# Transposes of the first and the last head on TensorE, and the gated output written over z

## The chip, the cores and the metric

The kernel runs on one core of one Trainium2 chip. What counts is the time of one execution on the device in microseconds (us). The number for the kernel before is the median of three runs.

## What is computed

One layer of a decoder for 1024 prompt rows and 8 decode rows, D = 1024, 8 heads of 128, in float32. Only the part that the change touches is shown; the rest (a conformer branch, a merge, a convolutional feed-forward) surrounds it.

```python
q, k, v = split_cols(silu(causal_dwconv(qkv)))
q = l2norm(q); k = l2norm(k)
def step(s, xc):                         # chunk after chunk, state s
    qg_c, kg_c, u_c, w_c, qk_c, gl_c = xc
    v_new = u_c - w_c @ s
    o = qg_c @ s + qk_c @ v_new
    s = s * gl_c + kg_c.T @ v_new
    return s, o
o = o * rsqrt(mean(o * o) + EPS) * delta_norm_w
o = o * silu(z)
y_a = o.reshape(b, t, V_DIM) @ w_o_delta
```

## The kernel before

The big products (`gemm`, its matmul at L187) run on TensorE (PE). Weights and activations are split in a high and a low float32r part, three products for each of eight k-slices, so a tile of 344 rows is 24 matmuls; three tiles make one projection of 128 columns. They go through two PSUM buffers `mm`. The projections come in a fixed order: for each head k, q, v (`kT`, `qT`, `vT`), with z, gate and conformer projections between; after head 7's the last z and gate projections; then the output projection of the gated heads, called wod here (`mm<-og`), which takes the split heads `og` as its moving operand, head by head along k.

PE runs in the order in which the program is written. VectorE (DVE), ScalarE (ACT), GpSimd (POOL) and SyncE (SP) run in an order that a scheduler makes. The work on the heads is written as background jobs, Python generators. `tick()` advances them all by a step after every four gemm matmuls, so `yield n` stands for 2n ticks, or 8n matmuls. Where the program must have a job's result (`wait_x`, `finish`), it ticks with no gemm between: such a place is called a bare stretch here.

The job of one head has these parts:

- `delta_a` (L645): the product of keys with themselves (L673), then a 32-step triangular solve on DVE (tiles `xt`, `xx`), whose result `xr` goes through DRAM (`d_x`) and comes back as `dt`. The generator then yields, 26 for head 0, 21 for heads 1 to 6, 14 for head 7.
- `delta_q` (L723): the product of queries with keys (L738) and the sum of squares of q over its columns.
- `delta_b` (L748): transposes of v and k, scaled into `vs` and `kt`; the inverse of a triangular matrix in blocks, of which the first (L776) needs `dt`; and the chain over the eight chunks (L819 to L844), which keeps one output tile `oo` for all heads and waits until the head before is "done".
- `delta_c` (L850): scales `oo`, transposes it, and multiplies it by silu(z) (`zT`) into `oo`; the result goes to DRAM (`d_og`). Head 7's is split at once for wod. A single buffer holds `zT`; the next head's z projection (`z_next`) waits for "done" too.

Four transposes of [128, 1024] for each head go through `flip` (L626): DVE turns blocks of 32x32 (a stream transpose) into tile `ty`, POOL sends it to DRAM (`d_t`), and four POOL transfers bring it back as `tv`. `ty` and `tv` share one buffer. PE's small products of these jobs use three PSUM buffers `tr`.

Of the kernel before, what the change touches and what calls it, by code (L numbers as in the profile page):

```python
# [8 lines left out]
F32 = mybir.dt.float32  # L9
# [7 lines left out]
P = 128  # L17
# [49 lines left out]
def body(tc, I, O):  # L67
# [13 lines left out]
    def stt(out, a, s, b, op0, op1):  # L81
        nc.vector.scalar_tensor_tensor(out=out, in0=a, scalar=s, in1=b, op0=op0, op1=op1)  # L82
# [5 lines left out]
    with top:  # L88
# [545 lines left out]
                nc.gpsimd.dma_start(tv[HB * b:HB * (b + 1)].rearrange("p (a x) -> p a x", a=4), dv[b])  # L634
            return tv.rearrange("p (a c s) -> p c a s", a=4, c=NC)

        def sumsq(src, ss):
            tv = flip(src)
            yield 3
            for c in range(NC):  # L640
                jk = hp.tile([P, P], F32, tag="jk", name="jk")
                nc.scalar.activation(jk.rearrange("p (a s) -> p a s", a=4), tv[:, c], AF.Square,
                                     accum_out=ss[:, c:c + 1])

        def delta_a(X):  # L645
# [71 lines left out]
            for b in range(4):  # L717
                nc.sync.dma_start(dt[HB * b:HB * (b + 1)].rearrange("p c r -> p (c r)"),
                                  d_x[:, b].rearrange("i c r -> i (c r)"))
            yield 14 if h == NH - 1 else 26 if h == 0 else 21  # L720
            X.update(dt=dt, d_x=d_x)

        def delta_q(X):  # L723
            h, kT, qT = X["h"], X["kT"], X["qT"]
            while "sc" not in X:
                yield
            pt = X["pt"]
            brk, c1, nc1g, rqs = X["sc"]
            gr2 = hp.tile([P, NC, P], F32, tag="gr", name="gr2")
            nc.sync.dma_start(gr2.rearrange("p c i -> p (c i)"),  # L730
                              d_gc[1, h * NC:(h + 1) * NC].rearrange("c i -> (c i)").unsqueeze(0).broadcast_to([P, T]))
            yield 3
            for half in range(2):
                g = trp()
                gv = g.rearrange("p (c i) -> p c i", i=P)
                for i in range(4):
                    c = half * 4 + i
                    nc.tensor.matmul(gv[:, i, :], kT[:, cs[c]], qT[:, cs[c]], start=True, stop=True)  # L738
                mul(pt[:, 4 * half:4 * half + 4, :], gv, pt[:, 4 * half:4 * half + 4, :])
                yield  # L740
            ss = hp.tile([P, NC], F32, tag="ss", name="ss")
            yield from sumsq(qT, ss)
            nc.vector.tensor_scalar(out=rqs, in0=ss, scalar1=EPS, scalar2=EPS / QS ** 2, op0=ALU.add, op1=ALU.mult)
            mul(qT, qT, gr2.rearrange("p c i -> p (c i)"))
            X.update(qdone=True)

        def delta_b(X):
# [5 lines left out]
            kt = hp.tile([P, NC, P], F32, tag="kt", name="kt")  # L753
            vs = hp.tile([P, NC, P], F32, tag="vs", name="vs")
            for src, dst, scl in ((vT, vs, brk), (kT, kt, eg[:, h, :])):
                tv = flip(src)
                yield 5
                for c in range(NC):
# [50 lines left out]
                nc.scalar.copy(tt[0:64, :, 64:128], t2v[0:64])  # L809
            X["merged"] = True  # L810
            yield 2
            while h > 0 and not Xs[h - 1].get("done"):
                yield
            S = None
            oo = hp.tile([P, NC, P], F32, tag="oo", name="oo")
# [34 lines left out]
        def delta_c(X):  # L850
# [11 lines left out]
            for c in range(NC):  # L862
                nc.scalar.activation(oo[:, c, :], oo[:, c, :], AF.Copy, scale=f[:, c:c + 1])
            yield 2
            tv = flip(oo.rearrange("p c i -> p (c i)"))
            yield 7
            zv, ov = zT.rearrange("p (c b r) -> p b c r", b=4, r=HB), oo.rearrange("p c (b r) -> p b c r", b=4)
            for b in range(4):
                stt(ov[:, b], tv[:, :, b], dnw, zv[:, b], ALU.mult, ALU.mult)
            if h == NH - 1:  # L870
                og = oo.rearrange("p c i -> p (c i)")
                for o in (0, 512):
                    split(oghi[h][:, o:o + 512], oglo[h][:, o:o + 512], og[:, o:o + 512])
            yield
            if h < NH - 1:
                nc.sync.dma_start(d_og[h], oo.rearrange("p c i -> p (c i)"))
            X["done"] = True

        def decode(h, sq_):
            nc.sync.dma_start(O["qs"][h], sq_)  # L880
# [849 lines left out]
```

## Time and profile before

| | us |
|---|---|
| median of three runs (lowest, highest) | 1848.58 (1846.51, 1850.22) |
| the profiled execution | 1842.05 |
| its span | 1840.3 |
| PE busy | 1774.9 |
| DVE busy | 1403.6 |
| ACT busy | 894.0 |
| POOL busy | 215.5 |

The busy times are those of one profiled execution; they overlap. PE is busy for 96% of the span, so what matters is when PE is idle, and for whom it waits. The profile gives for every instruction its start, its duration and, if its engine was idle before, for how long and what ended that. Matmuls overlap, so the step from one start to the next is PE's pace, not the duration of one.

### The profile page before, as it was taken

The page shows a single profiled execution, that of the slowest core. Times are in us where ns is not written, and L with a number is a line of the kernel's source. Part 1 is how long each engine was busy: PE and PEld are TensorE (multiplying, and loading weights), DVE is VectorE, ACT ScalarE, POOL GpSimd, SP SyncE. Part 2 cuts the span into 40 slices and gives each one's busy share as a digit, 9 for nine tenths or more (in the row PEclk, how much of TensorE's full clock was granted, in tenths as well). Part 3 has the DMA queues.
Part 4 walks back from the last instruction along what each step waited for, and adds up shares of the span by engine and source line. Part 5 has one row for each costly group of instructions (what it writes and reads, how often), then busy time and mean ns, then how long its engine had stood idle before and what let it go on. Part 6 is the DMA issues. An engine that isn't in the chain of part 4 may idle for free.

```text
span 1840.3 us, 35347 instructions
## 1 busy us (share of the span) xinstructions
PE 1774.9 (96%) x13075; PEld 1751.9 (95%) x13075; DVE 1403.6 (76%) x3296; ACT 894.0 (49%) x2110; POOL 215.5 (12%) x409
## 2 busy tenths in 40 slices
PE   7997999999999999989899998999999999999997
PEld 7897999999999999989899998999999999999997
DVE  7998699789978997745428578988778878856553
ACT  5564566565655656444203344444444445644432
POOL 5422121113021211100000000100000000100000
PEclk9999999999999999989999999999999999999998
DMA  4164345434544454544547732322222224767562
GB/s 165 59 181 141 92 128 168 147 119 144 153 144 122 143 171 149 159 132 147 184 140 228 239 114 94 108 81 72 90 76 75 87 75 150 241 211 227 169 184 84
DMA packets 161741, 257.38 MB, mean 140 GB/s; under 512 B 40544, under 2 KB 88992, under 8 KB 161568
## 3 DMA queue, kind: packets, MB, share of 16 engines
q1 hardware_dynamic: 143760, 213.10, 37.3%
q0 software_dynamic: 10752, 33.56, 5.8%
q10 hardware_dynamic: 7056, 8.47, 1.3%
q8 instruction: 102, 1.67, 0.4%
q14 instruction: 71, 0.58, 0.1%
HBM read 189.14 MB, written 65.92 MB: 139 GB/s over the span
## 4 chain that ended last, share of the span: by engine, by line
PE 66%; DVE 3%; DMA 2%; ACT 1%; issue 1%; SPq 0%; DVEq 0%; ACTq 0%
PE mm L187 25%; PE mm L1334 23%; PE mm L1599 13%; PE psS L834 0%; PE po L841 0%; DMA og<-d_og 0%; PE po L831 0%; PE pv L825 0%; DVE l_t L79 0%; PE pk L820 0%; PE nrm_b L224 0%; PE tr L673 0%; DMA yl<-d_y 0%; PE tr L738 0%; DMA d_ch<-c 0%
## 5 line engine op out<-in xcount | busy, mean ns | idle before, releaser
L187 PE MATMUL mm<-hhi,whi 128*128 128x344 f32 x1360 | 450.7, 331 | 11.9 <-ACT whi L85 6.6
L187 PE MATMUL mm<-hhi,wlo 128*128 128x344 f32 x1360 | 450.3, 331 | 2.7 <-DVE wlo L79 2.7
L187 PE MATMUL mm<-hlo,whi 128*128 128x344 f32 x1360 | 441.2, 330 | 0.0
L187 PEld LDWEIGHTS mm<-hhi,whi 128*128 128x128 f32 x1360 | 261.1, 192 | 16.1 <-ACT whi L85 7.0
L187 PEld LDWEIGHTS mm<-hhi,wlo 128*128 128x128 f32 x1360 | 261.3, 192 | 5.1 <-DVE wlo L79 3.9
L187 PEld LDWEIGHTS mm<-hlo,whi 128*128 128x128 f32 x1360 | 259.3, 192 | 0.5
L1334 PE MATMUL mm<-l_t,uhi 128*128 128x258 f32 x704 | 200.4, 285 | 1.4 <-DVE l_t L79 1.4
L1334 PE MATMUL mm<-h_t,uhi 128*128 128x258 f32 x704 | 200.4, 285 | 0.0
L1334 PE MATMUL mm<-h_t,ulo 128*128 128x258 f32 x704 | 199.4, 283 | 0.0
L82 DVE SCALAR_TENSOR_TENSOR cacc<-u,ccw,cacc 128x512 f32<-128x512 f32 x240 | 174.2, 744 | 0.5 <-ACT cacc L570 0.5
L1599 PE MATMUL mm<-yl,wdh 128*128 128x344 f32 x528 | 168.8, 320 | 0.0
L1599 PE MATMUL mm<-yh,wdh 128*128 128x344 f32 x528 | 168.8, 320 | 0.0
L1599 PE MATMUL mm<-yh,wdl 128*128 128x344 f32 x528 | 168.6, 319 | 0.0
L79 DVE TENSOR_TENSOR wdl<-draw,wdh 128x512 fp32r<-128x512 f32 x144 | 92.0, 646 | 81.4 <-ACT wdh L85 78.0
L145 ACT CAST whi<-wraw 128x512 fp32r<-128x512 f32 x164 | 95.7, 625 | 111.3 <-PE mm L187 93.9
L85 ACT CAST wdh<-draw 128x512 fp32r<-128x512 f32 x144 | 83.2, 584 | 111.8 <-PE mm L1599 103.2
L1334 PEld LDWEIGHTS mm<-l_t,uhi 128*128 128x128 f32 x704 | 133.9, 190 | 2.2 <-DVE l_t L79 2.2
L1334 PEld LDWEIGHTS mm<-h_t,uhi 128*128 128x128 f32 x704 | 133.6, 190 | 0.5 <-DVE u L79 0.2
L1334 PEld LDWEIGHTS mm<-h_t,ulo 128*128 128x128 f32 x704 | 133.5, 190 | 0.0
L187 PE MATMUL mm<-og,whi 128*128 128x344 f32 x512 | 124.6, 323 | 5.6 <-ACT og L85 5.6
L146 DVE TENSOR_TENSOR wlo<-wraw,whi 128x512 fp32r<-128x512 f32 x160 | 107.9, 688 | 13.9 <-ACT whi L145 12.6
L85 ACT CAST uhi<-s 128x512 fp32r<-128x512 f32 x92 | 56.9, 621 | 106.1 <-PE mm L1334 101.7
(356 smaller groups left out, 4287.7 us busy)
## 6 DMA issues: line engine op xcount, KB each, us to landing
draw<-in_wdn SPq DMA_DIRECT2D x120, 256.0 KB, 2.7
raw<-in_wup SPq DMA_DIRECT2D x92, 256.0 KB, 2.8
d_t<-ty POOLq DMA_DIRECT2D x32, 512.0 KB, 3.1
tv<-d_t POOLq DMA_DIRECT2D x128, 128.0 KB, 3.1
yl<-d_y SPq DMA_DIRECT2D x21, 516.0 KB, 5.5
d_y<-av SPq DMA_DIRECT2D x21, 512.0 KB, 3.1
gr<-d_gc SPq DMA_DIRECT2D x16, 512.0 KB, 3.5
wraw<-in_wout SPq DMA_DIRECT2D x32, 256.0 KB, 2.9
```

The lines of the kernel that those rows point to most:

```text
L79: nc.vector.tensor_tensor(out=out, in0=a, in1=b, op=ALU.subtract)
L82: nc.vector.scalar_tensor_tensor(out=out, in0=a, scalar=s, in1=b, op0=op0, op1=op1)
L85: nc.scalar.copy(hi, x)
L145: nc.scalar.copy(hi[:, k:k + 4], raw)
L146: weng["e"].tensor_tensor(out=lo[:, k:k + 4], in0=raw, in1=hi[:, k:k + 4].bitcast(F32), op=ALU.subtract)
L187: nc.tensor.matmul(ps, lhs[:, k, :], r(k), start=k == 0 and i == 0, stop=k == kt - 1 and i == 2)
L1334: nc.tensor.matmul(z[:, b, 0:Q], w[:, k, :], r[b][nm][:, k, :], start=start and n == 0, stop=n == 3 * KH - 1, skip_group_check=True)
L1599: nc.tensor.matmul(ps, w[:, f % KH, :], y[:, f % 3, :], start=h == 0 and n == 0, stop=h == 1 and n == 3 * (NF - 3 * KH) - 1)
```

## The change

Heads 0 and 7: the transposes of q, v, k and the gated output are PE transposes against the identity, into `tr` buffers (a new helper `turn`, four blocks of 128x128 for each half; the output in four quarters of two). ACT and DVE read them from PSUM. Heads 1 to 6 keep `flip`, but the gated output is written over `zT` and sent to DRAM from there. `oo` counts as free three yields after the flip was issued, and the next chain waits for "free" in place of "done". The yield at the end of `delta_a` is 2 longer for heads 1 to 7.

```diff
+        def turn(src):
+            for half in range(2):
+                g = trp()
+                gv = g.rearrange("p (c i) -> p c i", i=P)
+                for i in range(4):
+                    nc.tensor.transpose(gv[:, i, :], src[:, cs[half * 4 + i]], ident)
+                yield half, gv
+
-        def sumsq(src, ss):
+        def sumsq(src, ss, h):
+            if h in (0, NH - 1):
+                for half, gv in turn(src):
+                    for i in range(4):
+                        c = half * 4 + i
+                        jk = hp.tile([P, P], F32, tag="jk", name="jk")
+                        nc.scalar.activation(jk, gv[:, i, :], AF.Square, accum_out=ss[:, c:c + 1])
+                    yield 2
+                return
             tv = flip(src)
             yield 3
...
-            yield 14 if h == NH - 1 else 26 if h == 0 else 21
+            yield 16 if h == NH - 1 else 26 if h == 0 else 23
...
             for src, dst, scl in ((vT, vs, brk), (kT, kt, eg[:, h, :])):
+                if h in (0, NH - 1):
+                    for half, gv in turn(src):
+                        for i in range(4):
+                            c = half * 4 + i
+                            nc.scalar.activation(dst[:, c, :], gv[:, i, :], AF.Copy, scale=scl[:, c:c + 1])
+                        yield
+                    X["vt"] = True
+                    continue
                 tv = flip(src)
                 yield 5
...
-            while h > 0 and not Xs[h - 1].get("done"):
+            while h > 0 and not Xs[h - 1].get("free"):
                 yield
...
-            tv = flip(oo.rearrange("p c i -> p (c i)"))
-            yield 7
-            zv, ov = zT.rearrange("p (c b r) -> p b c r", b=4, r=HB), oo.rearrange("p c (b r) -> p b c r", b=4)
-            for b in range(4):
-                stt(ov[:, b], tv[:, :, b], dnw, zv[:, b], ALU.mult, ALU.mult)
-            if h == NH - 1:
-                og = oo.rearrange("p c i -> p (c i)")
-                for o in (0, 512):
-                    split(oghi[h][:, o:o + 512], oglo[h][:, o:o + 512], og[:, o:o + 512])
-            yield
+            if 0 < h < NH - 1:
+                tv = flip(oo.rearrange("p c i -> p (c i)"))
+                yield 3
+                X["free"] = True
+                yield 4
+                zv = zT.rearrange("p (c b r) -> p b c r", b=4, r=HB)
+                for b in range(4):
+                    stt(zv[:, b], tv[:, :, b], dnw, zv[:, b], ALU.mult, ALU.mult)
+                yield
+                nc.sync.dma_start(d_og[h], zT)
+                X["done"] = True
+                return
+            for qr in range(4):
+                g = trp()[:, 0:256]
+                gv = g.rearrange("p (c i) -> p c i", i=P)
+                for i in range(2):
+                    c = qr * 2 + i
+                    nc.tensor.transpose(gv[:, i, :], oo[:, c, :], ident)
+                og = oo[:, 2 * qr:2 * qr + 2, :].rearrange("p c i -> p (c i)")
+                sl = slice(256 * qr, 256 * qr + 256)
+                stt(og, g, dnw, zT[:, sl], ALU.mult, ALU.mult)
+                if h == NH - 1:
+                    split(oghi[h][:, sl], oglo[h][:, sl], og)
+                yield
             if h < NH - 1:
                 nc.sync.dma_start(d_og[h], oo.rearrange("p c i -> p (c i)"))
-            X["done"] = True
+            X["free"] = X["done"] = True
```

The new rows on PE are 64 transposes. Counted in gemm matmuls issued so far, of which 4104 precede wod, head 0's stand at 476 and 492 (q), 516 and 524 (v), 532 and 540 (k), and 1132 to 1156 (output); head 7's at 3500 and 3516, 3656 and 3664, 3672 and 3680, and 4072, 4080, 4088 and 4096. L776 and the chain of heads 1 to 6 stand 16 matmuls later than before; L776 of heads 0 and 7 stands where it was.

Three places show how the change moves work. The first is DVE at the end of head 0's triangular solve. The fence is the order before; `xr` is the solve's result, `qT`, `vT`, `jk` and `am` belong to head 1, `Sb` to the decode rows.

```order
L73 TENSOR_TENSOR xt_1303<-ab_1236,xx_1241 128x24
L677 SCALAR_TENSOR_TENSOR jk_1984,ss_1931<-tr_1979,const_71 128x128
L79 TENSOR_TENSOR xx_1241<-xx_1241,xt_1303 128x24
L82 SCALAR_TENSOR_TENSOR Sb_1181<-Sb_1181,adec_106,vb_1743 128x128
L73 TENSOR_TENSOR xt_1303<-ab_1236,xx_1241 128x16
L677 SCALAR_TENSOR_TENSOR jk_1986,ss_1931<-tr_1979,const_71 128x128
L79 TENSOR_TENSOR xx_1241<-xx_1241,xt_1303 128x16
```

And the same place in the changed kernel:

```order
L73 TENSOR_TENSOR xt_1307<-ab_1236,xx_1241 128x8
L79 TENSOR_TENSOR xx_1241<-xx_1241,xt_1307 128x8
L729 COPY xr_1617<-xx_1241 128x256
L82 SCALAR_TENSOR_TENSOR qT_1814<-raw_1903,cqw_84,qT_1814 128x344 x3
L693 SCALAR_TENSOR_TENSOR jk_1940,ss_1934<-tr_1935,const_71 128x128
```

The products `jk` of head 1 stood between the last steps of the solve; now they, and three of head 1's `qT` steps, stand behind `xr`. Between the first step of the solve and `xr` 17 instructions fewer are left: 7 `jk`, 6 `qT`, 1 `vT`, 4 `cacc` (conformer convolution), the stream transpose of k, an `am` and a `pt` are gone from there, and 4 small ones have come in. Ahead of the first step little changes: the stream transposes of q and v and 2 `wlo` are gone, 4 `cacc` and a `pt` have come in.

The second place is PE where head 7's chain begins, at the start of the last z projection (a bare stretch). Before:

```order
L795 MATMUL tr_10263<-const_71,tt_123 64x64 x8
L797 MATMUL tr_10264<-tt_123,am_9065 64x64 x8
L807 MATMUL tr_10289<-z2_10282,t1_10281 64x64 x8
L187 MATMUL mm_10311<-hhi0_78,whi_9868 128x344
L187 MATMUL mm_10311<-hhi0_78,wlo_9869 128x344
```

And in the changed kernel:

```order
L819 MATMUL tr_10272<-const_71,tt_123 64x64 x8
L821 MATMUL tr_10273<-tt_123,am_9041 64x64 x8
L831 MATMUL tr_10294<-z2_10291,t1_10290 64x64 x8
L849 MATMUL pv_10310<-vs_9989,tt_123 128x128
L187 MATMUL mm_10327<-hhi0_78,whi_9862 128x344
```

The chain's first product `pv` stood 12 gemm matmuls further on; now it follows at once on the product whose copy `tt` it reads. On ACT the copies `oo<-po` of chunk 0 stood behind the second `zT<-mm` of this projection and now stand ahead of the first; those of chunk 1 stood behind the second and now stand behind the first.

The third place is DVE ahead of wod, where head 7's gated output is made. Before:

```order
L82 SCALAR_TENSOR_TENSOR c_10733<-c_10733,ccv_86,tr_11104 128x258 x4
L146 TENSOR_TENSOR wlo_11144<-wraw_11145,whi_11143 128x512
L146 TENSOR_TENSOR wlo_11144<-wraw_11149,whi_11143 128x512
L593 COPY c_11128<-cdec_104 128x4x8
L82 SCALAR_TENSOR_TENSOR oo_10324<-tv_11091,dnw_87,zT_10300 128x8x32 x4
L79 TENSOR_TENSOR og_10937<-oo_10324,og_10936 128x512 x2
```

And in the changed kernel:

```order
L79 TENSOR_TENSOR og_10926<-oo_10308,og_10925 128x256
L82 SCALAR_TENSOR_TENSOR oo_10308<-tr_11132,dnw_87,zT_10316 128x256
L79 TENSOR_TENSOR og_10926<-oo_10308,og_10925 128x256
L146 TENSOR_TENSOR wlo_11152<-wraw_11153,whi_11151 128x512
L146 TENSOR_TENSOR wlo_11152<-wraw_11157,whi_11151 128x512
L593 COPY c_11173<-cdec_104 128x4x8
```

The multiplications by silu(z) stood behind a copy into `c` (conformer); all four quarters now stand ahead of it.

## Rows read from the trace of the kernel before

**Rows 1.** The page's first part, for one engine: busy time, its share of the span, instructions.

```profile
PE 1774.9 (96%) x13075; PEld 1751.9 (95%) x13075; DVE 1403.6 (76%) x3296; ACT 894.0 (49%) x2110; POOL 215.5 (12%) x409
```

**Rows 2.** PE's waits over the whole span: the line that waited, what it waited for, us in total, times, the longest.

```profile
PE tr L776 <- DMA dt<-d_x: 12.6, 4, 9.4
...
PE po L831 <- ACT oo L844: 6.0, 2, 5.1
PE mm L187 <- ACT og L85: 5.6, 1, 5.6
```

**Rows 3.** One window of 25 us at head 0's first wait: its length, busy time and instructions of PE, weight loads, DVE, ACT and POOL, then the granted clock (1 is 2.4 GHz, 0.5 is 1.2 GHz), the DMA engines' share and GB/s.

```profile
175.00:200.00 25.00, 19.06 (x186) 17.59 (x187) 12.74 (x42) 14.03 (x50) 2.92 (x8) 0.80 0.41 121
```

**Rows 4.** The timeline of PE around head 0's L776 and the start of its chain: start, us, engine, line, operation, how many, and in brackets the idle time before and what ended it.

```profile
169.57 0.32 PE L187 MATMUL mm<-hhi,wlo 128*128 128x344 f32 x1
169.72 0.32 PE L187 MATMUL mm<-hlo,whi 128*128 128x344 f32 x1
179.45 1.39 PE L776 MATMUL tr<-dt,am 32*32 32x32 f32 x32 [9.40 <-DMA dt<-d_x]
...
181.22 0.49 PE L187 MATMUL mm<-hhi,wlo 128*128 128x344 f32 x1
...
184.66 0.49 PE L187 MATMUL mm<-hhi,wlo 128*128 128x344 f32 x1
...
188.78 0.63 PE L795 MATMUL tr<-const,tt 64*64 64x64 f32 x8
...
193.38 0.49 PE L825 MATMUL pv<-vs,tt 128*128 128x128 f32 x2 [0.99 <-ACT tt L809]
193.71 1.06 PE L738 MATMUL tr<-qT,kT 128*128 128x128 f32 x8
194.60 0.39 PE L834 MATMUL psS<-vn,kt 128*128 128x128 f32 x2
```

**Rows 5.** The timeline of DVE and of SP's queue on the way to head 0's `dt`: the three stream transposes, the solve's result, and the loads of `dt`.

```profile
98.49 1.23 DVE L629 STREAM_TRANSPOSE ty<-qT 128x1024 f32<-128x1024 f32 x1
...
118.45 1.25 DVE L629 STREAM_TRANSPOSE ty<-vT 128x1024 f32<-128x1024 f32 x1
...
136.22 1.25 DVE L629 STREAM_TRANSPOSE ty<-kT 128x1024 f32<-128x1024 f32 x1 [1.70 <-ACT vs L759]
...
170.65 0.38 DVE L713 COPY xr<-xx 128x256 f32<-128x256 f32 x1
...
175.78 2.28 SPq L718 DMA_DIRECT2D dt<-d_x  x4
```

**Rows 6.** The timeline around the start of head 7's chain, all engines: head 6's gated output on DVE and SP, the chain on PE, ACT's copies.

```profile
776.16 0.98 ACT L863 ACTIVATE oo<-oo,f 128x128 f32<-128x128 f32 x3
...
788.06 1.25 DVE L629 STREAM_TRANSPOSE ty<-oo 128x1024 f32<-128x1024 f32 x1 [4.45 <-ACT kt L759]
...
800.88 0.40 PE L187 MATMUL mm<-hhi,whi 128*128 128x344 f32 x1
801.12 0.32 PE L187 MATMUL mm<-hhi,wlo 128*128 128x344 f32 x1
...
803.13 1.14 ACT L957 CAST og<-og 128x512 fp32r<-128x512 f32 x2 [5.11 <-DMA og<-d_og]
...
803.23 1.67 DVE L82 SCALAR_TENSOR_TENSOR oo<-tv,dnw,zT 128x256 f32<-128x256 f32 x4
...
803.28 0.39 PE L825 MATMUL pv<-vs,tt 128*128 128x128 f32 x2
...
804.92 0.32 SPq L876 DMA_DIRECT2D d_og<-oo  x1
...
808.05 0.28 ACT L843 ACTIVATE oo<-po 128x128 f32<-128x128 f32 x1 [0.97 <-DMA d_og<-oo]
...
808.77 0.79 PE L831 MATMUL po<-S,qT 128*128 128x128 f32 x2 [5.10 <-ACT oo L844]
...
809.65 0.49 PE L187 MATMUL mm<-hhi,wlo 128*128 128x344 f32 x1
...
813.08 0.36 PE L187 MATMUL mm<-hhi,wlo 128*128 128x344 f32 x1
```

**Rows 7.** The timeline at the start of wod, PE and DVE: the last matmul ahead of the wait, what DVE did, the first matmul behind it.

```profile
875.63 0.32 PE L187 MATMUL mm<-og,whi 128*128 128x344 f32 x1
...
879.03 0.18 DVE L593 COPY c<-cdec 128x32 f32<-128x32 f32 x1 [3.14 <-DMA d_ch<-c]
...
879.21 1.67 DVE L82 SCALAR_TENSOR_TENSOR oo<-tv,dnw,zT 128x256 f32<-128x256 f32 x4
...
881.59 0.66 PE L187 MATMUL mm<-og,whi 128*128 128x344 f32 x1 [5.64 <-ACT og L85]
...
884.77 0.36 PE L187 MATMUL mm<-og,wlo 128*128 128x344 f32 x1
```

**Rows 8.** Groups by line and form over the whole span: line, engine, operation, form and count, then busy us, mean ns of one, idle time before.

```profile
L759 ACT ACTIVATE vs<-tv,sc 128x128 f32<-128x128 f32 x64 | 21.3, 397 | 2.2 <-DMA tv<-d_t 2.2
...
L920 PE MATMUL tr<-const,vnd 128*8 128x128 f32 x8 | 2.2, 272 | 0.0
```

**Rows 9.** PE's waits at L776 in the windows 300 to 400 and 600 to 700, the columns as in rows 2.

```profile
PE tr L776 <- DMA dt<-d_x: 0.8, 1, 0.8
...
PE tr L776 <- DMA dt<-d_x: 2.5, 2, 2.0
```

More of the change, by code (lines that the diff above doesn't have):

```diff
@@ L741, in delta_q @@
             ss = hp.tile([P, NC], F32, tag="ss", name="ss")
-            yield from sumsq(qT, ss)
+            yield from sumsq(qT, ss, h)
             nc.vector.tensor_scalar(out=rqs, in0=ss, scalar1=EPS, scalar2=EPS / QS ** 2, op0=ALU.add, op1=ALU.mult)
```

## The prediction

> **What bounds the kernel now.** I read the page's first part, then PE's waits, then the timeline around the longest of them, then DVE, ACT and the queues there. PE is busy for 96% of the span [rows 1], so the change can gain only where PE waits or runs slowly, and loses wherever it gives PE work. Three waits are within reach of the change: one of 9.40 us for head 0's `dt`, one of 5.10 at `po` for ACT's copy of `oo`, one of 5.64 for head 7's split output; beside the 9.40, L776 waits 3.2 in all [rows 2], for later heads [rows 9].
>
> Behind each wait PE runs slowly for a while. Behind the first, the gemm's step is 0.287 us (181.22 to 184.66, 12 steps), against 0.15 to 0.16 ahead of it (169.57 to 169.72), and L776 takes 1.39; the granted clock of that window is 0.80 [rows 3, 4]. The step at half speed, 0.287, less the full one, 0.158, makes 0.129 lost on each matmul. Between the wait and the return of full speed stand some 14 matmuls behind the first wait, 10 behind the second (809.65 to 813.08, with three chain products) and 11 behind the third (to 884.77) [rows 4, 6, 7]. So the waits cost more than their length.
>
> **Stall 1: head 0's `dt`.** `dt` is `xr` sent out and loaded again: `xr` at 170.65, the loads issued from 175.78, L776 free at 179.45 [rows 4, 5]. PE was done with its gemm at about 170.0, so `dt` must come 9.4 us sooner, or PE come later. Both happen. Between the first step of the solve and `xr` DVE loses 21 instructions and gains 4 small ones, by the order. DVE has no gap there but the 1.70 us at the stream transpose of k, which waits for ACT to free the one `ty` buffer [rows 5]. That stream transpose takes 1.25, the gap goes with it; the other 20 at an estimated 0.45 each (from 1.25 for 1024 columns [rows 5], and 0.3 to 0.6 for a quarter or half of that) make 9; the four small ones give back about 0.8. Sum: 1.25 + 1.70 + 9 − 0.8, about 11 us sooner. The lower bound counts the stream transposes and the gap alone, 1.23 + 1.25 + 1.25 + 1.70 = 5.4; below that, nothing, if DVE is held elsewhere. I take 11, since the order shows where the rest went: behind `xr`. On its side PE has head 0's six halves of q, v and k to do first, about 3.1 us (below). `dt` then lands at about 168.5, PE comes at 173.1: the wait is gone with 4.6 us of margin. Gain: 9.40 + 0.7 (L776 takes 1.39 against an estimated 0.7 at full speed) + 14 × 0.129 = 1.8, together **11.9**. What is late next on PE is the chain's own copy wait of 0.99 at 193.38 [rows 4], which stays.
>
> **The transposes on PE.** Twelve halves of four and eight quarters of two, 64 blocks. The nearest row is eight records of f32 products of the same size, 193.71 to 194.60, 0.111 us each; such a product of two records between gemm matmuls also delays the next one, whose step is 0.24 (800.88 to 801.12) in place of 0.158, so 0.08 for each group [rows 4, 6]. A transpose in this kernel has one record where a product has two (L920, one for each head) [rows 8]. So a half costs 4 × 0.111 + 0.08 = 0.52, a quarter 0.30: 12 × 0.52 + 8 × 0.30 = **8.7** (6.2 + 2.4). The upper bound is two records each, 64 × 0.111 = 7.1 more. A floor lies at 64 × 0.07 (the eight transposes of 64 columns take 0.56 or so [rows 4]): 2.6 less. I take 8.7, since the columns are 128.
>
> The halves also need buffers: three `tr` in turn, freed by ACT's four reads of each half at about 0.40 [rows 8], 1.6 us; two halves stand 8 matmuls apart, 1.27 + 0.52 = 1.8 us, for v and k. ACT just keeps up where it has nothing else to do. Bounds: nothing, to 12 × 1.6 = 19. I take **2**, since two buffers stand between a half and its reuse.
>
> **Stall 2: head 6's output and head 7's chain.** The 5.10 at 808.77 has this history: ACT's `oo<-po` waits until `d_og<-oo` has been sent (issued 804.92, ACT free at 808.05), that waits for `oo<-tv` at 803.23, and the stream transpose of `oo` ran only at 788.06 because head 7's k held the `ty` buffer (4.45 idle for ACT's `kt`) [rows 6]. The change takes away each link: head 7's k no longer uses `ty`; `oo` is read last by the stream transpose; and chunk 0's copies stand ahead of `zT<-mm` on ACT. Gone: 5.10 + 10 × 0.129 = 1.3 + about 0.7 for L831, L834 and L841 at half speed: **7.1**. Against it, head 7's `pv` now follows at once on L831's product and waits for ACT's copy `tt`; the same wait for head 0 is 0.99 [rows 4]: **1.0** lost. What is queued behind it on PE is the whole z projection.
>
> `zT` is now what is held: until `d_og<-zT` has been sent, 3.1 us from issue to ACT's release [rows 6]. The scale of head 6's `oo` ended at 777.1, and comes 16 matmuls later by the order, 2.5 us: 779.6. The stream transpose follows at once, or where DVE came to it before, 788.06 less its 4.45 idle, 783.6, and 2.5 later: 786.1. From there to the multiplication it was 15.2 us (788.06 to 803.23), and 1.7 + 3.4 more free `zT`: 799.9 to 806.4. PE needs the first of its two `mm` buffers back for the third z tile; that stood at the `pv` of chunk 1, 803.28 [rows 6], and now 1.0 later. So PE waits 0 to 2.6; I take **1.0**. ACT's cast of `og`, which waited 5.11 for its load at 803.13 [rows 6], stands ahead of chunk 1's `vn`; that may cost 0 to 2.
>
> **Stall 3: wod.** The 5.64 at 881.59 is for `og` of head 7; DVE's multiplication at 879.21 stood in line behind the copy L593, which waited 3.14 for `d_ch<-c` [rows 7]. In the new order all four quarters stand ahead of L593, and the last PE quarter 8 matmuls ahead of wod, 29 matmuls or 4.6 us ahead of the first use. Gone: 5.64 + 11 × 0.129 = **7.0**. L593 now holds only the evacuation of wod's first tile; for that, and for a late quarter, I take **1.0** off, bounds 0 to 2.
>
> **Heads 1 to 6.** Their L776 stands 16 matmuls later, 2.5 us; the waits of 0.8 and of 2.5 in two pieces [rows 9] are covered almost wholly: **3.0**, bounds 0 to 5 with the clock behind them. The chain's later start costs nothing there: the next head's z comes long after.
>
> **Sum.** 11.9 + 7.1 − 1.0 − 1.0 + 7.0 − 1.0 + 3.0 = 26.0 gained, 8.7 + 2 = 10.7 lost: 15.3 in all. From the profiled execution that is 1842.05 − 15.3 = 1826.8. This execution was 6.5 us below the median of the runs, which is the number that counts: 1848.58 − 15.3 = **1833**.
>
> **A rule on the clock.** Behind the eight transposes at 188.78 the products run at 0.111 each, as at full speed [rows 4]. The Trainium skill (TensorE: Matmul & The Clock Gate, Part 4: PE-mode transpose) says that a transpose does not count as busy for the clock as a product does, and gives some 275 ns for one in a kernel; 64 such end to end would be an estimated 17.6 us in place of 8.7, and the sum 1842. By the trace it doesn't hold for eight blocks of 64 columns; for groups of four blocks of 128 no row shows it.
>
> **The rivals.** First, `zT` takes the place of `oo`: `d_og<-zT` lands after 809, ACT holds chunk 1's copies behind `zT<-mm`, and stall 2's net 5.1 is not gained: 1838. For it, the length of the path from the stream transpose (15.2); against it, the span worked out above, which ends before. Second, head 0's `dt` comes no sooner, because DVE is held by something ahead of the solve: then PE's 3.1 us go into the wait for nothing and the 11.9 aren't gained, 1833 + 8.8 = 1842. For it, DVE's order ahead of the solve hardly changes; against it, 21 instructions gone behind. Third, the clock falls at the turns of heads 0 and 7: 64 matmuls from the first to the last of head 0's and 24 of head 7's v and k at 0.129 make 11.4: 1845. Fourth, the slower side: the `tr` buffers bind. ACT answers each half only after PE has come to the third buffer on, 12 × 1.6 = 19 in place of 2, and a transpose takes two records, 7 more: 1833 + 24 = 1857. It decides where ACT's reads of a half come more than about 3.6 us late (two halves on PE); ACT's wait of 5.11 for `og` shows that it can be that late, but that place is not at a turn. That the change would not do what it says is shut out by the order, which has the 64 rows and the moved chain.
>
> **How the numbers follow.** The sum 0.50, first rival 0.17, second 0.13, third 0.05, fourth 0.10, and the first and second together 0.05 (1847). What a measurement of this kernel can tell from no change is about 0.2%, 3.7 us. The sum's own range is 1828 to 1838 from its bounds. The range reaches from 1825 (no wait for buffers, all of stall 3, more clock) to 1845, which leaves out the fourth case and half of the doubled one. Faster: 0.50 + 0.17 + 0.13 and half of the third make 0.82, less a little for the spread of each, 0.79; same 0.10 (the third, the doubled one and that spread); slower 0.11.
>
> **What would show it.** Right: no wait at L776 for head 0 and a granted clock near 1 there; head 7's `po` and wod's eighth head with no wait over 1 us; transposes of 128 columns one record each at about 0.11. Wrong: PE waiting at a transpose for ACT or DVE, `zT<-mm` on ACT waiting for `d_og<-zT`, or a new wait of PE for `vn`.

## The result, and the profile after

The changed kernel takes 1818.8 us, the median of four runs (1814.67 to 1819.69), against 1847.55 for the kernel before (four runs, 1843.89 to 1850.22). The ratio is 0.9841, with a 95% interval of 0.9818 to 0.9865: 25 to 34 us faster. In the experiments, with more runs of the kernel before, the same two kernels gave 0.9865 (0.9846 to 0.9883) and 0.9869 (0.9850 to 0.9889). The forecast was 1833, the range 1825 to 1845: the direction was right, the gain nearly twice the one forecast.

The page's first part, after, against [rows 1]. The span is 22.4 us shorter and PE's busy time only 1.1, although 64 instructions came in: most of what went is idle time, and the rest is slow running behind the waits.

```profile
PE 1773.8 (98%) x13139; PEld 1751.1 (96%) x13139; DVE 1399.4 (77%) x3290; ACT 892.8 (49%) x2112; POOL 188.7 (10%) x369
```

PE's waits over the whole span, after: line, what it waited for, us in total, times, longest. Of [rows 2] the waits for `oo` and for `og` are gone, and that for `dt` (L776, now L800) has shrunk from 12.6 us in four pieces to one of 0.5. What is left in the stretch that the change edits is small and has other causes, most of it ACT's copies of `vn` and `tt` in the chain. The larger waits that the view lists besides, 6.7 for `whi` and 4.9 for `nrm_r`, lie outside that stretch and stood there before.

```profile
PE psS L858 <- ACT vn L852: 2.6, 4, 1.0
...
PE pv L849 <- ACT tt L833: 1.7, 2, 1.0
...
PE tr L809 <- DVE rk L82: 0.9, 1, 0.9
...
PE tr L800 <- DMA dt<-d_x: 0.5, 1, 0.5
```

The timeline of PE, after: a half of head 0's v, turned ahead of gemm matmuls, then L800 of head 0. Four transposes of one record each start 0.11 apart from 118.68 on ((0.60 − 0.27) / 3, with the 0.27 of one record from [rows 8]). The next matmul starts at 119.04, only 0.03 behind the fourth, and its own step is 0.24 in place of 0.16. L800 has no wait (9.40 in [rows 4]) and lasts 0.69 in place of 1.39. The next product, L809, waits 0.94 for DVE.

```profile
118.52 0.32 PE L187 MATMUL mm<-hlo,whi 128*128 128x344 f32 x1
118.68 0.60 PE L642 MATMUL tr<-const,vT 128*128 128x128 f32 x4
119.04 0.40 PE L187 MATMUL mm<-hhi,whi 128*128 128x344 f32 x1
119.28 0.32 PE L187 MATMUL mm<-hhi,wlo 128*128 128x344 f32 x1
...
173.40 0.69 PE L800 MATMUL tr<-dt,am 32*32 32x32 f32 x32
...
177.74 0.69 PE L809 MATMUL tr<-zs,xs 32*32 32x32 f32 x32 [0.94 <-DVE rk L82]
```

Two windows of PE, after: length, busy time and instructions, granted clock, DMA share, GB/s. The first holds head 0's turns of q, v and k (the last ends at 124.4), the second is that of [rows 3], where the clock was 0.80. Both show 1.00.

```profile
109.00:124.00 15.00, 15.00 (x107) 1.00 0.53 155
...
175.00:200.00 25.00, 21.79 (x197) 1.00 0.46 134
```

DVE and SP's queue on the way to head 0's `dt`, after, to be read against [rows 5]: `xr` at 164.14 in place of 170.65, and the loads issued at 168.21 in place of 175.78.

```profile
164.14 0.42 DVE L729 COPY xr<-xx 128x256 f32<-128x256 f32 x1
...
168.21 1.71 SPq L734 DMA_DIRECT2D dt<-d_x  x4
```

The start of head 7's chain, after, against [rows 6]. The stream transpose of head 6's `oo` runs at 770.86, 17.2 us earlier than before (8.1 earlier counted from head 7's L795, which PE reached at 789.33 and now at 780.22), and waits for the scale on ACT, not for `kt`. The multiplication now writes `zT`, and ACT's first `zT<-mm` waits 0.83 for its sending. PE's `po` has no wait; `pv` waits 0.67 for `tt`.

```profile
770.86 1.25 DVE L629 STREAM_TRANSPOSE ty<-oo 128x1024 f32<-128x1024 f32 x1 [1.75 <-ACT oo L887]
...
784.42 0.80 PE L849 MATMUL pv<-vs,tt 128*128 128x128 f32 x2 [0.67 <-ACT tt L833]
...
788.26 1.27 DVE L82 SCALAR_TENSOR_TENSOR zT<-tv,dnw,zT 128x256 f32<-128x256 f32 x3
...
789.55 0.32 SPq L898 DMA_DIRECT2D d_og<-zT  x1
...
792.42 0.39 PE L855 MATMUL po<-S,qT 128*128 128x128 f32 x2
...
794.95 0.46 ACT L529 ACTIVATE zT<-mm 128x344 f32<-128x344 f32 x1 [0.83 <-DMA d_og<-zT]
```

A short slow stretch stays where this chain begins: the clock was granted at half from about 784 to 787 (0.94 over the window 784 to 809), much as from 793 to 796 before. What is gone is the second one, behind the wait at `po`.

The start of wod, after, against [rows 7]: the last quarter's transposes at 855.28, its low part on DVE at 856.66, wod's first matmul with no wait behind it, and the copy L593, which held head 7's output up, behind all of that.

```profile
855.28 0.38 PE L906 MATMUL tr<-const,oo 128*128 128x128 f32 x2
...
856.66 0.42 DVE L79 TENSOR_TENSOR og<-oo,og 128x256 fp32r<-128x256 f32 x1 [0.47 <-ACT og L85]
...
856.77 0.32 PE L187 MATMUL mm<-og,whi 128*128 128x344 f32 x1
...
859.62 0.18 DVE L593 COPY c<-cdec 128x32 f32<-128x32 f32 x1 [0.36 <-DMA d_ch<-c]
```

### The profile page after: what moved, and what is told of

Read it like the earlier page. It is cut to its first block, busy times and chain, and to the rows that moved or that the text cites. A ratio compares the mean times of both kernels' runs of the same rounds, so it can differ in the third digit from the quotient of the medians.

```text
span 1817.9 us, 35374 instructions
## 1 busy us (share of the span) xinstructions
PE 1773.8 (98%) x13139; PEld 1751.1 (96%) x13139; DVE 1399.4 (77%) x3290; ACT 892.8 (49%) x2112; POOL 188.7 (10%) x369
## 4 chain that ended last, share of the span: by engine, by line
PE 85%; DVE 8%; DMA 3%; ACT 2%; issue 1%; SPq 0%; DVEq 0%; ACTq 0%
PE mm L187 41%; PE mm L1372 23%; PE mm L1637 13%; PE psS L858 1%; PE tr L689 1%; PE pv L849 1%; PE po L865 1%; PE pk L844 1%; PE tr L754 1%; PE po L855 1%; DVE xt L82 1%; DMA yl<-d_y 1%; DMA wraw<-in_wout 0%; PE tr L821 0%; PE tr L947 0%
## 5 line engine op out<-in xcount | busy, mean ns | idle before, releaser
L187 PE MATMUL mm<-hhi,whi 128*128 128x344 f32 x1360 | 448.7, 330 | 10.9 <-ACT whi L85 6.7
```

The lines of the kernel that those rows point to most:

```text
L187: nc.tensor.matmul(ps, lhs[:, k, :], r(k), start=k == 0 and i == 0, stop=k == kt - 1 and i == 2)
```

## The experiments

To see where the time went, each profile was cut at points on PE that have the same number of gemm matmuls ahead of them in both kernels. The touched stretch runs from the first product of keys (L673, 95.53 us before) to the first matmul of the conformer's projection (972.58). No edit stands in the program ahead of it or behind it; those parts are called the untouched stages. A head's decode product is the one of its decode rows with ones (`tr<-s,ones`, L895 before). In us, first profiles:

| stretch on PE | before | after | gain | forecast |
|---|---|---|---|---|
| first keys product to head 1's decode product (stall 1, head 0's q, v, k) | 101.89 | 93.65 | 8.2 | 8.8 |
| to head 2's decode product (head 0's output) | 103.20 | 103.44 | -0.2 | -1.2 |
| to head 7's decode product (heads 1 to 6, head 7's q) | 444.21 | 439.89 | 4.3 | 2.0 |
| to the start of head 7's chain, L795 (head 7's v, k) | 44.50 | 46.92 | -2.4 | -2.1 |
| to wod (stall 2, head 7's output) | 83.16 | 76.54 | 6.6 | 3.9 |
| to the conformer's projection (stall 3) | 100.09 | 92.66 | 7.4 | 6.0 |
| touched stretch | 877.05 | 853.10 | 23.9 | 17.4, less 2 for buffers |
| untouched, ahead and behind | 963.25 | 964.80 | -1.5 | 0 |

The variants are the changed kernel with sets of heads in place of its fixed ones: TQ (q, v, k turned on PE), TO (output turned on PE), ZS (stream transpose, output over z); other heads go as before. In the changed kernel these are heads 0 and 7, heads 0 and 7, and heads 1 to 6; the yields are 16 and 23 (before 14 and 21). Head 0 alone, head 7 alone and the write into z alone have the old yields.

```diff
-                if h in (0, NH - 1):
+                if h in TQ:
...
-            if 0 < h < NH - 1:
+            if h in ZS:
                 tv = flip(oo.rearrange("p c i -> p (c i)"))
...
+            if h not in TO:
+                tv = flip(oo.rearrange("p c i -> p (c i)"))
+                yield 7
...
+                X["free"] = X["done"] = True
+                return
```

**The kernel before, a second time** (no edit).

> The kernel before, unchanged, profiled once more. In the two profiles on hand the change gained 22.4 us (spans 1840.3 and 1817.9), but in the medians 28.7. Theory A: the first profiled execution of before was a short one, and others wait longer at the same places (dt of head 0, oo, og), since these waits end with transfers; then this profile shows a span nearer 1846 and the waits of 9.4, 5.1 and 5.6 longer by some 5 us in sum. Theory B: executions differ elsewhere, in places that the change does not touch; then the three waits are within 0.5 us of what they were, whatever the span. Ratio to before 1.000 +- 0.002 in both.

Ratio 1.0001 (0.9989 to 1.0012), span 1844.2. The waits for `dt`, `oo` and `og` were 9.44, 5.64 and 5.13 us, against 9.40, 5.10 and 5.64: two moved by 0.5, one up and one down, and the sum by 0.1. The touched stretch took 875.2 us, the untouched stages 969.0. So the span differs where the change touches nothing, as theory B had it; what that means for the sum is taken up with the last runs.

**Head 0 alone.**

```diff
+TQ = (0,)
+TO = (0,)
+ZS = ()
```

> Only head 0 is turned on TensorE (q, v, k and the output); all else as before, the old yields and the wait for done too. From the two profiles: up to head 1's first products the change gained 8.5 us net, and lost 1.4 at head 0's output. Theory A (terms add, each at its place): 7 us gained, ratio 0.996; the wait for dt of head 0 gone, the waits of 5.1 and 5.6 unchanged within 1 us. Rival: what head 0 gains is given back further on, since DVE has the displaced work to do behind the solve and keeps the later heads late: gain under 3 us, with new waits for DVE between 200 and 700.

Ratio 0.9952 (0.9935 to 0.9969), 1837.8 us. The wait for `dt` of head 0 is gone, `po` waits 5.38 and wod 6.17, as theory A had it. But part of the rival was seen too: counted from the first keys product, the gain was 8.3 us at head 1's decode product and 5.4 at head 7's. The product that takes `dt` (L776 before, L804 here) waited 2.09, 0.94 and 2.14 us at heads 4 and 6, with the old yields.

**Head 7 alone.**

```diff
+TQ = (7,)
+TO = (7,)
+ZS = ()
```

> Only head 7 is turned on TensorE (q, v, k and the output); heads 0 to 6 as before, with the output in oo, and the chain waits for done. Theory A: the wait at po came from the one buffer of ty and tv, which head 7's k held from 769.9 to 788; with that gone the stream transpose of head 6's output runs some 8 us sooner, and the wait goes without the output being put into z. Gain 7.1 + 7.0 - 4.3 for the 40 transposes, some 9 us, ratio 0.995. Rival: the write into z is what removes the wait (oo is held until it has been sent), so here 3 us or more of it stay: gain 4 to 6 us.

Ratio 0.9921 (0.9906 to 0.9935), 1831.4 us. The touched stretch is 867.1 us, 10.0 below that of the first profile. DVE, SP and PE of this run: the stream transpose of `oo` at 781.07 has no wait, and `po` waits 0.78 although `oo` is still sent before it is free.

```profile
781.07 1.25 DVE L633 STREAM_TRANSPOSE ty<-oo 128x1024 f32<-128x1024 f32 x1
...
801.61 0.32 SPq L917 DMA_DIRECT2D d_og<-oo  x1
...
805.25 0.49 PE L859 MATMUL po<-S,qT 128*128 128x128 f32 x2 [0.78 <-ACT oo L872]
```

So the wait at `po` goes when head 7's q, v and k leave the shared buffer; the write into z is not needed for it. That it is k which matters is seen in the run with 16 transposes fewer. The whole time fell by more than the touched stretch, as in other runs below.

**The write into z alone.**

```diff
+TQ = ()
+TO = ()
+ZS = (1, 2, 3, 4, 5, 6)
```

> Only the gated output of heads 1 to 6 is put into z's buffer and the next chain waits for free; all transposes as before, the old yields. Theory A: head 7's k still holds the buffer, the stream transpose of head 6's output comes as late as before, z's buffer is sent at about 805 and the wait at po becomes one for z's buffer, of 3 us or more: gain 0 to 3 us, ratio 0.998 to 1.000. Rival: the write into z removes the wait by itself: gain 5 to 7 us, ratio 0.996 to 0.997.

Ratio 1.0002 (0.9991 to 1.0013): no gain. In its profile the touched stretch took 873.8 us, 3.2 below the mean of four profiles of the kernel before, and the untouched stages 969.1, 2.7 above theirs. DVE and PE of this run: the stream transpose comes as late as before, 4.44 behind `kt`, the multiplication at 802.41, and PE waits 4.16 us at a gemm matmul for `zT<-mm` in place of 5.10 at `po`. That is the prediction's first rival, seen where the buffer isn't free.

```profile
787.90 1.25 DVE L633 STREAM_TRANSPOSE ty<-oo 128x1024 f32<-128x1024 f32 x1 [4.44 <-ACT kt L787]
...
802.41 1.66 DVE L86 SCALAR_TENSOR_TENSOR zT<-tv,dnw,zT 128x256 f32<-128x256 f32 x4
...
807.23 0.66 PE L191 MATMUL mm<-hhi,whi 128*128 128x344 f32 x1 [4.16 <-ACT zT L533]
```

**The later yields alone** (16 and 23 in the kernel before).

> Only the yields at the end of delta_a are longer (16 for head 7, 23 for heads 1 to 6); all transposes, oo and the wait for done as before. Theory A: L776 of heads 1 to 6 comes 2.5 us later, so its waits (0.8, 2.0, 0.5) and the slow clock behind them go: gain 2 to 4 us, ratio 0.998 to 0.999. Rival: the chain comes later too and is late for z or for the next head, in new waits of PE for ACT or DVE: ratio 1.000 or above.

Ratio 0.9992 (0.9983 to 1.0001): 1.5 us, with an interval from 3.1 faster to 0.2 slower, so not told from nothing. Between head 2's and head 7's decode products it took 437.5 us, 6.7 less than before; from there to wod 131.1 against 127.7, and wod waited 5.15 and then 1.32. The gain was made and given back at head 7, whose later chain met the two stalls that this variant keeps.

**The changed kernel with the old yields.**

```diff
-            yield 16 if h == NH - 1 else 26 if h == 0 else 23
+            yield 14 if h == NH - 1 else 26 if h == 0 else 21
```

> The changed kernel with the old yields (14 and 21). Theory A: heads 1 to 6 wait for dt again, and more than before, since head 0 no longer holds PE up: 4 to 7 us slower than the changed kernel, some 1823 to 1826 us, ratio to before 0.987 to 0.989. Rival: the yields do nothing: 1819 us, 0.985.

Ratio 0.9885 (0.9868 to 0.9901), 1824.5 us, within what theory A gave. PE of this run at heads 4 and 6: waits for `dt` of 1.24, 0.97 and 2.47, more than in [rows 9].

```profile
515.32 0.24 PE L804 MATMUL tr<-dt,am 32*32 32x32 f32 x2 [1.24 <-DMA dt<-d_x]
...
692.22 0.24 PE L804 MATMUL tr<-dt,am 32*32 32x32 f32 x2 [0.97 <-DMA dt<-d_x]
...
694.93 1.05 PE L804 MATMUL tr<-dt,am 32*32 32x32 f32 x30 [2.47 <-DMA dt<-d_x]
```

The stretch from head 2's to head 7's decode product took 449.3 us here and 439.9 in the changed kernel: without head 0's stall PE comes sooner to the next heads' `dt`, and in these two profiles the yields take 9.5 us out of that stretch, not 3. Of these, 1.9 come back on the way to head 7's chain (44.99 here, 46.91 in the changed kernel). By the runs the yields are worth some 4 us of the whole (0.9885 here, 0.9865 and 0.9869 for the changed kernel, with intervals that overlap); this profile was the slowest of its four runs.

The touched stretch took 861.0 us, 16.0 below the mean of the kernel before. Head 0 alone took 6.0 off it and head 7 alone 10.0, so with the old yields these two add.

**The changed kernel without the write into z** (ZS empty).

> The changed kernel without the write into z: heads 1 to 6 keep their output in oo, and the chain waits for done. Theory A (the buffer of ty was the cause of the wait at po): the stream transpose of head 6's output comes early, and this loses 0 to 3 us against the changed kernel, 1819 to 1822 us, ratio to before 0.985 to 0.987. Rival: with the later yields the chain of head 7 needs oo early, and the wait at po is back with 4 us or more: 1823 us or above.

Ratio 0.9868 (0.9848 to 0.9888), 1820.6 us, the touched stretch 854.4. `po` waits 1.82. From L795 of head 7 to wod it took 78.2 us in place of 76.5, so the write into z is worth 1.6 us there, as theory A had it. In the runs it is not told from nothing (0.9865 and 0.9869 for the changed kernel).

**Head 7's q, v and k by stream transposes in the changed kernel** (TQ only head 0).

> The changed kernel with head 7's q, v and k turned by stream transposes again (24 transposes fewer on TensorE, 3.1 us); head 7's output and all of head 0 stay on TensorE. Theory A: head 7's k holds the buffer of ty again, z's buffer is sent late, and PE waits for it 4 us or more at the last z projection, as in the run with the write into z alone (4.16): 1820 to 1823 us, ratio to before 0.985 to 0.988. Rival: the write into z is enough, and only the 3.1 us are seen: 1816 us, 0.983.

Ratio 0.9900 (0.9882 to 0.9919), 1828.0 us: theory A by its sign and its wait, and slower than its number. In its profile the touched stretch is 859.2, 5.7 above the changed kernel's mean, and the untouched stages 968.4, 4.0 above. DVE and PE of this run: `oo` waits 4.81 for `kt` again, and PE 5.04 for `zT<-mm`.

```profile
776.65 1.25 DVE L633 STREAM_TRANSPOSE ty<-oo 128x1024 f32<-128x1024 f32 x1 [4.81 <-ACT kt L787]
...
799.33 0.65 PE L191 MATMUL mm<-hhi,whi 128*128 128x344 f32 x1 [5.04 <-ACT zT L533]
```

**The changed kernel, a second time** (no edit).

> The changed kernel, unchanged, profiled once more, with more rounds. From the first profiles, cut at points with the same number of gemm matmuls: between the first product of keys and the first matmul of the conformer's projection it needs 853.1 us, before 877.1 (and 875.2 in its second profile); all other stages together 964.8, before 963.3 and 969.0. Theory A: the 24 us are the change's, and repeat within 1 us; the other stages scatter between executions, from 962 to 970, whatever the kernel. Rival: the other stages are shorter for the changed kernel in most executions, since their transfers fall otherwise. Ratio 0.984 to 0.987 by both.

Ratio 0.9865 (0.9846 to 0.9883). Touched stretch 852.7, untouched stages 964.4.

**All heads on TensorE** (TQ and TO all heads, ZS empty).

> All eight heads turned on TensorE, 192 transposes more than in the changed kernel. Theory A (0.111 us each and 0.08 for each group, as six heads times 6 x 0.52 + 4 x 0.30): 26 us more on PE than in the changed kernel, and nothing given back, since PE waits there for only some 3 us: 1843 to 1846 us, ratio 0.998 to 1.000. Rival (two records each): 1860 us. Second rival: ACT answers too late for the three tr buffers and PE waits at the transposes for 0.5 us or more a half: 1860 us or above, with such waits in the profile.

Ratio 0.9950 (0.9933 to 0.9966), 1835.1 us, faster than every theory gave. The touched stretch took 870.5 us, 17.4 more than the changed kernel's for 192 transposes more. By the steps of the profile after, a half of four costs 0.36 + 0.24 − 0.16 = 0.44 us and a quarter of two 0.22, so 36 halves and 24 quarters make 21.1. PE's waits that the views list in the touched stretch fell from 7.7 us to 3.7, which makes up the difference. PE's waits in this run between 90 and 1000 us, all that the view lists: of the 256 transposes of this edit one waits, an output's, for 0.5.

```profile
PE tr L603 <- DVE cscr L80: 1.4, 1, 1.4
PE pv L853 <- ACT tt L837: 1.0, 1, 1.0
PE psS L862 <- ACT vn L856: 0.8, 2, 0.5
PE tr L925 <- ACT c L613: 0.5, 1, 0.5
```

**24 transposes fewer** (head 0: only q, v, k on TensorE; head 7: only k and the output; heads 0 to 6 write into z).

> The changed kernel with 24 transposes fewer: head 0's output by a stream transpose and written into z as in heads 1 to 6, and of head 7 only k and the output on TensorE, q and v by stream transposes. Theory A: only k has to keep out of the buffer of ty and tv for the last z projection, so nothing waits anew, and 2.1 + 1.2 = 3.3 us less stand on PE: 3 us below the changed kernel, ratio 0.983. Rival: head 7's v still holds the buffer when k's place comes, or holds up k's and v's copies on ACT: the wait at the last z projection is back, 2 us or more above the changed kernel.

Ratio 0.9859 (0.9845 to 0.9874), 1819.1 us, beside 0.9865 for the changed kernel in the same set of runs: not told apart. The touched stretch is 849.9 us, 2.8 below the changed kernel's, as theory A had it. From the conformer's projection to the feed-forward it took 148.7 us in place of 146.0. PE's waits in this run there, where 1.6 for `whi` stood at 0.2 in the changed kernel:

```profile
PE mm L193 <- DVE wlo L152: 1.9, 2, 1.6
PE mm L193 <- ACT whi L151: 1.6, 1, 1.6
PE mm L193 <- DVE sgb L88: 0.9, 1, 0.9
```

So in these profiles the merge stage gave the gain back: it waits for its weights. Why they aren't there sooner when PE is, was not tried.

**16 transposes fewer** (as the one before, with head 0's output on TensorE).

> As the run with 24 fewer, but head 0's output stays on TensorE, so 16 transposes fewer than the changed kernel. Theory A: 2.1 us below the changed kernel, ratio 0.983. Rival: q's and v's stream transposes of head 7 hold the buffer, and the last z projection waits again.

Ratio 0.9857 (0.9840 to 0.9874). This run differs from the one with head 7's q, v and k by stream transposes in head 7's k alone, and the wait of 5.04 there is gone here: PE waits neither at `po` nor for `zT`. So head 7's k in the shared buffer was the cause. The touched stretch is 856.1, 3.4 above the changed kernel's: L800 of head 4 waited 2.05 for `dt`, where it waited 0.30 to 1.32 in three profiles of the changed kernel. Neither theory had that.

**Three more profiles**, two of the kernel before and one of the changed kernel, and 24 transposes fewer with a yield of 25.

> The kernel before, a third profile. Theory A (executions differ by themselves in the untouched stages): those stages together take anything from 962 to 970 us, the touched stretch 875 to 877. Theory B (the kernel before is slower there as a rule): 966 us or above again, with the wait of 1.9 us or more at the final norm's product near 1665 and the slow clock behind it.

> The kernel before, a fourth profile, the same two readings as of the third.

> The changed kernel, a third profile. Theory A: untouched stages anywhere from 962 to 970 us, touched stretch 853 within 0.5. Theory B: untouched stages 965 or below again, the wait at the final norm's product under 1.2 us.

> The run with 24 transposes fewer, with the yield of heads 1 to 6 at 25 in place of 23. Theory A: the waits for dt are gone already, so nothing is left to gain, and the chain's copies of vn (waits of 0.5 to 0.95) only move: within 1 us of that run, 1818 to 1820 us. Rival: later chains push the last z projection's wait back in: 2 us or more above.

Ratios 1.0000, 1.0007 and 0.9869 (0.9850 to 0.9889), and 0.9867 (0.9850 to 0.9883) for the yield of 25, which does nothing, as theory A had it. The four profiles of the kernel before have touched stretches of 877.1, 875.2, 878.2 and 877.7 us, mean 877.0, and untouched stages of 963.3, 969.0, 965.2 and 967.9, mean 966.3. The three of the changed kernel have 853.1, 852.7 and 854.8, mean 853.5, and 964.8, 964.4 and 964.1, mean 964.4. So 23.5 us are the change's, in the stretch that it edits, and 1.9 more lie outside it, less than the scatter of the kernel before there. Neither theory holds whole: the kernel before scatters over 6 us outside, with the first profile at its low end, and the changed kernel over 1 us. Not all of it is scatter: the merge stage took 145.6 to 146.1 us in the changed kernel's profiles (146.9 to 148.1 before), and the up projection of the feed-forward (L1334 before) 452.8 to 453.1 (451.3 to 451.6 before). These ranges do not touch, one a gain and the other a loss; what causes either was not looked for.

One place of that scatter is in the rows. At a product of the final norm PE waits for DVE's chain `nrm_x`, `nrm_r`: 1.13 us in the first profile of before, 2.74 in the fourth, 0.78 to 1.12 in the changed kernel. PE of the fourth profile, the wait, and the window of 25 us behind it, with its granted clock of 0.93 (1.00 in the first profile's):

```profile
1668.03 1.15 PE L224 MATMUL nrm_b<-const,nrm_r 128*128 128x128 f32 x6 [2.74 <-DVE nrm_x L210]
```

```profile
1665.00:1690.00 25.00, 22.26 (x133) 0.93 0.76 228
```

From that product on, twenty records of PE took 4.5 us in the fourth profile and 3.0 in the first. The down projection around it took 256.6 us in the fourth and 253.4 in the first.

## Why the prediction was too small

**The mechanisms held, each at its place.** Head 0's wait for `dt`, the wait at `po` and the wait at wod are gone, each with the slow clock behind it. Head 0 alone, head 7 alone, the 16 transposes fewer and the old yields show which edit removed which.

The first rival (z takes the place of `oo`) was seen where head 7's k keeps the buffer, in two runs, and not in the changed kernel. The second (`dt` no sooner) did not come about, though `xr` came 7.3 us sooner, counted from the first keys product, and not 11: the margin of 4.6 us was in truth about 1.5 (168.21 plus the 3.7 from issue to use in [rows 4, 5] make 171.9, and PE came at 173.40). Counted in the same way the loads were issued 8.4 us sooner, 1.0 less than the wait of 9.40, so by this estimate `dt` alone would have left some of it: PE's own 2.6 us of transposes ahead of that place covered the rest, which the prediction had as a second cause.

The third rival was the clock. By the rows of the profile after the clock stays at 1.00 through head 0's turns (and from 758 to 770, at head 7's of v and k), and the next matmul starts 0.36 us after the first of four transposes. The rule of the Trainium skill (TensorE: Matmul & The Clock Gate, Part 4: PE-mode transpose), that the full clock does not engage for transposes, is not borne out here, where groups of two and four stand between gemm matmuls; for transposes by themselves no run shows it. The 275 ns that the Trainium skill gives there for one of bf16 is near the duration of an f32 record in this trace (272 ns), and far from what one costs PE (0.111 us).

The fourth (the `tr` buffers bind) is refuted by the run with all heads on TensorE.

**The sizes failed, nearly all on the same side.** Of the 8.6 us that the touched stretch of the first profiles gained beyond the forecast of 15.3:

- Transposes: 8.7 forecast, 12 × 0.44 + 8 × 0.22 = 7.0 measured. The step from record to record, 0.111, was right. The 0.08 added for each of the 20 groups was counted twice: the next matmul starts 0.03 behind the last record and not 0.111, and its longer step only makes that up. The kernel before shows it (the fence below): from 800.58 to 801.12 are 0.54 us, which is two steps of 0.158 and 0.22 for a product of two records, where the prediction's way of counting gives 0.30.
- The `tr` buffers: 2 forecast, nothing measured.
- Heads 1 to 6: 3.0 forecast; measured 4.3 with 0.9 of head 7's q paid, so 5.2. The step priced the waits of before alone. The later yields alone took 6.7 off that stretch, so what stands behind these waits (the slow clock, and a wait of 1.39 at L785, which the later yields removed) was left out, and so was the growth of the waits once head 0's stall was gone.
- Stall 2: 5.1 forecast. From L795 to wod 6.6 was gained with head 7's output, 0.9, paid, so 7.5. The wait for `zT` (1.0 forecast) did not come, `pv` waits 0.67 and not 1.0, and a wait of 0.94 for a gate's copy, which no term had, went too. (The 3.4 in that stall's path is 3.1 by [rows 6]; only its bounds rest on it.)
- Stall 3: 6.0 forecast, 7.4 measured: the 1.0 taken off for L593 and a late quarter was not lost.
- Stall 1: 11.9 forecast; 8.2 with 2.6 of transposes paid makes 10.9. L809 waits 0.94 for DVE now.

These make 1.7 + 2.0 + 2.2 + 2.4 + 1.4 − 1.0 = 8.7. Two stages that had no term but their transposes moved too, head 0's output by 0.6 for the better and head 7's v and k by 0.7 for the worse; that they cancel is luck.

PE of the kernel before, around a product of two records; the two matmuls behind it are in [rows 6]:

```profile
800.58 0.32 PE L187 MATMUL mm<-hlo,whi 128*128 128x344 f32 x1
800.74 0.38 PE L820 MATMUL pk<-S,kT 128*128 128x128 f32 x2
```

**The step from one profile to the median failed too.** The sum was made against a profile 6.5 us below the median of three runs, and the difference was carried over to the changed kernel. That kernel's profile lies 0.9 above its median, and in the later sets, with 7 to 19 runs each, the median of the kernel before is 1844.0 to 1846.4, not 1848.6. The profile had untouched stages 3.1 us below the mean of four profiles. With 8.6, less 1.5 that the untouched stages differed in the first pair, and 7.4 of this offset the 14.5 us between 1833.3 and 1818.8 are accounted for.

**Open:** why the changed kernel's untouched stages scatter less, and lie 1.9 us lower in the mean. The wait at the final norm is one place. Head 7 alone had 962.5 and head 7's q, v and k by stream transposes 968.4, so neither head 0's transposes nor transposes as such decide it.

## What to carry to other kernels

A stall that a shared buffer causes is found by asking what the late instruction waited for, and for whom that one waited; here head 7's k was the cause of a wait at head 7's `po`, two buffers away. When one stall goes, price the next ones anew: the waits for `dt` of the later heads grew as soon as PE came sooner. The same two yields were worth about nothing alone (the touched stretch 0.9 us shorter) and 7.5 us of that stretch in the changed kernel. Cost terms that are each taken on the careful side add up to a sum that the result can miss with its whole range, so set them at what the nearest row says and leave the care to the range. And when a row prices an instruction between others, take the whole step from the neighbour ahead to the neighbour behind, so that nothing is counted twice.

## What was not expected of the hardware

Between gemm matmuls of 344 columns a transpose or product of 128 columns in f32 costs 0.111 us for each record, and the group costs nothing beside: the next matmul starts 0.03 behind the last record and then takes a step of 0.24 (118.68 to 119.28 after, 0.44 for four records; 800.58 to 801.12 before, 0.22 for two). A transpose has one record and a product two.

A wait of PE in a stage that no edit touches can cost more than its own length. At one product of the final norm PE waited 2.74 us in place of 1.13, 1.6 more; the granted clock behind it was 0.93 over 25 us in place of 1.00, and the down projection took 3.2 us longer.
